# Two looks for the largest scores at a time, in the first and third of every four attention slots of an encoder kernel

## The chip, the cores and the metric

The kernel runs on one core of one Trainium2 chip. The metric is the time of one execution in device microseconds; a kernel's time is the median of several runs. The profiler records one execution with every instruction of the five engines: PE (TensorE), PEld (PE's weight loads), DVE (VectorE), ACT (ScalarE), POOL (GpSimd), and SP, which issues the DMAs.

## The reference, cut to what matters

One layer of a bidirectional encoder is run on two sequences, a prompt of 1024 tokens and a sample of 2048, with width 1024. Behind a normalised input projection stand a pooling mixer, self-attention (8 heads of 64 on 2 key/value heads) and cross-attention (4 heads into 256 memory tokens). Their gated outputs go through one output projection, are normalised and added to x.

```python
def one_block(qblk):
    s = jnp.einsum('bqkgd,bskd->bkgqs', qblk, k, preferred_element_type=jnp.float32) * scale
    p = jax.nn.softmax(s, axis=-1)
    return jnp.einsum('bkgqs,bskd->bqkgd', p.astype(v.dtype), v)
...
mix = jnp.concatenate([pool_out, attn_out, x_out], axis=-1)
y = jnp.einsum('bte,ed->btd', mix, w_out)
return x + rms_norm(y, norm_post)
```

The query and key gains are large, so the softmax needs the largest score of each query before the exponentials are taken.

## The kernel before

The first part (some 700 us) computes all projections and stores queries, keys, values and gates in DRAM. The second part, which the change touches, does attention and output projection. It works through **pairs** of 128-query tiles: 8 pairs of the sample, then 4 of the prompt. A pair has three **groups**, one for each kind: kind 0 and kind 1 are the two key/value heads of self-attention, kind 2 is cross-attention. The order in a pair is 0, 2, 1 (2, 0, 1 in the first). A group goes through its keys in chunks of 128: 16 chunks for self-attention of the sample, 8 for the prompt, 2 for cross-attention. One chunk of one group is a **slot**; there are 344, and `k` is the chunk's number in its group.

PE, ACT, DVE and POOL run in the order in which the loop at the end of the kernel writes the instructions. A slot writes:

- `weights(k, 0)`: the scores S of 512 queries, transposed (keys on partitions), by two matmuls, first from `qa`, then from `qb` (line 220), the second of which also subtracts each query's largest score; ACT takes the exponential P (line 227). S comes from the PSUM pool `pss` with two buffers, P from a pool of six.
- `sums` of the slot before: P is added to the running z, for the sample one half on POOL (line 239) and one on DVE (line 240), for the prompt all of it on DVE.
- one **look** (`largest`, line 191, or 183 for cross-attention): for a later group, the scores of 128 queries against 1024 keys (queries on partitions) go into a buffer N of the PSUM pool `psn`, which has two buffers of 1024 numbers, and DVE reduces it to the negated largest (line 194). 324 looks lie in slots, 20 more in the first part. The last look of a group must be over more than LEAD = 4 slots ahead of the group.
- what is `due` at the slot; `weights(k, 1)` for the other 512 queries; some matmuls of the output projection, if there are any to fill in (`py`, lines 359 to 361); and what is due at the slot plus END = 0.5.

Every fourth slot the **value products** of four chunks stand at the slot's end (`values`, line 252, 16 matmul records): at k = 4, 8, 12 and at the first slot of the next group. Behind a group's last chunk follow, in the slots of the next: `values` at the end of its first slot, `totals` at the end of its second (line 260: the sums of z go into a buffer of `psn`, the same two as the looks'), `take` in its third (line 266: acc times the gate, on DVE) and `inverse` at the end of its third (line 272: DVE reads the totals' buffer, which is held until then).

The lines that set this for the looks and the totals:

```python
psn = ctx.enter_context(tc.tile_pool(name="psn", bufs=2, space=PSUM, side="right", reuse_waits="tile"))
...
at(n + c + 1 + END, g.totals)
at(n + c + 2, g.take)
at(n + c + 2 + END, g.inverse)
```

Here `n` is the group's first slot and `c` its number of chunks.

Of the kernel before, what the change touches and what calls it, by code (L numbers as in the profile page):

```python
# [23 lines left out]
def encoder(ctx, tc, I, O):  # L24
# [375 lines left out]
    LEAD, RUN = 4, 4  # L400
    pairs = [Pair(s, p) for s in (1, 0) for p in range(SEQS[s][1] // 256)]
    groups = []
# [5 lines left out]
    slots = [(g, k) for g in groups for k in range(g.chunks)]  # L408
# [3 lines left out]
    def at(slot, f, *args):  # L412

        later.setdefault(slot, []).append((f, args))

    def due(slot):
        for f, args in later.pop(slot, ()):
            f(*args)  # L418

    first = {}  # L420
# [18 lines left out]
    for g in groups:  # L439
        n, c = first[g], g.chunks  # L440
# [11 lines left out]

    looks, n = {}, len(slots)
    left = {g: list(range(len(g.pieces))) for g in groups}
    while any(left.values()):
        n -= 1
        able = [g for g in groups if left[g] and first[g] - LEAD > n]
        if able:  # L460
            looks[n] = (able[0], left[able[0]].pop())
    ahead = [looks[n] for n in sorted(looks) if n < 0]
    loads = {}
    for n, (g, k) in looks.items():
        if k == 0:
            loads.setdefault(max(n - 3, -1), []).append(g)

    order = {mybir.EngineType.PE, mybir.EngineType.Activation, mybir.EngineType.DVE,
             mybir.EngineType.Pool}

    def look_ahead():

        if ahead:
            g, n = ahead.pop(0)
            g.largest(n)


    with ExitStack() as p1:
# [334 lines left out]
        def groups_of(sb):  # L813
            return mem_groups if SB[sb][0] == "mem" else tok_groups
# [10 lines left out]
        for sb, (kind, s, nb, b0) in enumerate(SB):  # L825
            groups = groups_of(sb)
# [50 lines left out]
    with tc.manual_schedule(engines=order):  # L877
        slot = 0
        while slot < len(slots) or later or fill:
            g, k = slots[slot] if slot < len(slots) else (None, 0)  # L880
            if g:
                g.weights(k, 0)
            if 0 < slot <= len(slots):
                h, kh = slots[slot - 1]
                h.sums(kh)
            for x in loads.get(slot, ()):
                x.load()
            if slot in looks:
                looks[slot][0].largest(looks[slot][1])
            due(slot)  # L890
            if g:
                g.weights(k, 1)
            pauses = sum(x is None for x in fill)
            n = -(-(len(fill) - pauses) // max(1, until[0] - slot - pauses)) if fill else 0
            for _ in range(n):
                x = fill.pop(0)
                if x is None:
                    break
                out, h, c, start, final = x
                out.piece(h, c, start, final)  # L900
                if final:
                    if h == 0 and not out.last:

                        for n in sorted(later):
                            for x in [x for x in later[n] if x[0].__name__ in ("square", "norm", "out")]:
                                later[n].remove(x)
                                x[0](*x[1])
                    at(slot + END, out.half_out, h)
                    at(slot + 1 + END, out.square, h)
                    if h == 1:  # L910
                        at(slot + 2, out.norm)
                        at(slot + 3, out.out)
            due(slot + END)
            slot += 1

# [41 lines left out]
```

## Time and profile before

| | us |
|---|---|
| median of 3 runs (1882.11 to 1884.48) | 1884.24 |
| profiled execution: span from first to last instruction | 1878.7 |
| what lies around the span, by the median | 5.5 |
| second part, from its first S | 699.1 to 1878.7 |
| mean granted TensorE clock | 0.994 |

In the rows of the profile a line (L220) and a tile's name say what an instruction is. "Idle before" is the time for which its engine had nothing to do just ahead of it, with what ended it. A matmul's end is modelled, and matmuls overlap: in a stream, one of 512 columns starts about 0.23 us after the one before, though each shows about 0.40 us. So distances between starts are read here, not durations. One value product of float32 shows as two records.

### The profile page before, as it was taken

To read this page: it belongs to the slowest core of one execution; us is meant where nothing else is said; L and a number is where in the kernel's file an instruction comes from. 1 tells how busy PE (TensorE), PEld (TensorE's weight loads), DVE (VectorE), ACT (ScalarE), POOL (GpSimd) and SP (SyncE) were. 2 spreads that over 40 slices of the span, in tenths; PEclk is the share of its full clock that TensorE was granted. 3 is DMA by queue.
4 is the path that set the end of the run, shared out by engine and by line. 5 is a ranking of instruction groups with operands and counts; after the bars stand their busy time and mean duration, and the time that the engine had idled before them with its cause. 6 is when DMAs were issued, how large, how long until landed. Compare 5 with 4: busy or idle time off the path is not lost. (4 is left out here: it accounts for less than half of the span.)

```text
span 1878.7 us, 23531 instructions
## 1 busy us (share of the span) xinstructions
PE 1813.4 (97%) x8520; PEld 1279.4 (68%) x8520; DVE 1135.6 (60%) x1312; ACT 696.8 (37%) x1266; POOL 846.5 (45%) x748
## 2 busy tenths in 40 slices
PE   7999999999999999999999999999999999999997
PEld 6888888988988884465564656556465655565564
DVE  7745145431544168867768576776858576757744
ACT  5523234222422115444435344443434343333331
POOL 3655016520446007845638374563837452413311
PEclk9999999999999999999999999999999999999998
DMA  7634454254434926212122221212222153223211
GB/s 244 201 113 120 108 162 132 73 154 116 121 99 114 216 65 173 73 27 79 48 79 62 68 62 29 80 45 79 63 68 63 51 137 78 96 85 96 87 43 62
DMA packets 148485, 181.83 MB, mean 97 GB/s; under 512 B 21504, under 2 KB 118416, under 8 KB 148368
## 3 DMA queue, kind: packets, MB, share of 16 engines
q1 hardware_dynamic: 148368, 180.33, 33.9%
q8 instruction: 67, 1.10, 0.3%
q14 instruction: 50, 0.41, 0.1%
HBM read 126.50 MB, written 53.62 MB: 96 GB/s over the span
## 5 line engine op out<-in xcount | busy, mean ns | idle before, releaser
L227 ACT ACTIVATE P<-S 128x512 f32<-128x512 f32 x688 | 399.3, 598 | 555.5 <-PE S L220 430.8
L194 DVE TENSOR_REDUCE nb<-N 128x1 f32<-128x1024 f32 x256 | 311.7, 1218 | 239.8 <-PE N L191 239.0
L239 POOL TENSOR_TENSOR z<-z,P 128x512 f32<-128x512 f32 x224 | 318.4, 1421 | 222.5 <-ACT P L227 217.4
L252 PE MATMUL acc<-P,V 128*64 128x512 f32 (+1 forms) x1472 | 319.4, 576 | 0.5
L220 PE MATMUL S<-qa,KA 128*128 128x512 f32 x640 | 274.6, 429 | 9.7 <-ACT P L227 9.7
L63 POOL TENSOR_TENSOR rs<-rs,mhalf 128x1 f32<-128x1 f32 (+2 forms) x100 | 101.0, 1013 | 401.8 <-DVE rs L61 401.8
L240 DVE TENSOR_TENSOR z<-z,P 128x512 f32<-128x512 f32 (+1 forms) x272 | 271.0, 996 | 13.1 <-ACT P L227 12.9
L220 PE MATMUL S<-qb,KB 65*128 65x512 f32 x640 | 254.0, 397 | 0.0
L550 PE MATMUL pz<-hT_hi,w_hi 128*128 128x512 f32 x592 | 233.1, 394 | 1.3 <-ACT vmst L808 0.8
L552 PE MATMUL pz<-hT_hi,w_lo 128*128 128x512 f32 x592 | 232.1, 392 | 0.5 <-DVE w_lo L69 0.5
L551 PE MATMUL pz<-hT_lo,w_hi 128*128 128x512 f32 x592 | 232.3, 392 | 0.0
L191 PE MATMUL N<-KA,qa 128*128 128x512 f32 x640 | 207.5, 405 | 17.9 <-DVE rz L272 11.2
L252 PEld LDWEIGHTS acc<-P,V 128*64 128x64 f32 x1472 | 98.3, 138 | 178.7 <-issue 169.6
L220 PEld LDWEIGHTS S<-qa,KA 128*128 128x128 f32 x640 | 120.4, 188 | 143.9 <-issue 72.6
L194 DVE TENSOR_REDUCE top<-N 128x1 f32<-128x1024 f32 (+1 forms) x88 | 107.0, 1219 | 94.3 <-PE N L191 74.5
L191 PEld LDWEIGHTS N<-KA,qa 128*128 128x128 f32 x640 | 116.6, 191 | 60.9 <-DVE nb L194 21.9
L550 PE MATMUL pz<-w_hi,hT_hi 128*128 128x384 f32 (+1 forms) x416 | 140.2, 338 | 0.9 <-ACT hT_hi L68 0.8
L551 PE MATMUL pz<-w_lo,hT_hi 128*128 128x384 f32 (+1 forms) x416 | 139.4, 335 | 0.8 <-DVE w_lo L69 0.8
L552 PE MATMUL pz<-w_hi,hT_lo 128*128 128x384 f32 (+1 forms) x416 | 139.7, 338 | 0.0
L359 PE MATMUL py<-wo_hi,mix 128*128 128x512 f32 x352 | 137.7, 391 | 0.0
L360 PE MATMUL py<-wo_lo,mix 128*128 128x512 f32 x352 | 137.7, 391 | 0.0
L361 PE MATMUL py<-wo_hi,mix 128*128 128x512 f32 x352 | 137.4, 390 | 0.0
(120 smaller groups left out, 2479.5 us busy)
## 6 DMA issues: line engine op xcount, KB each, us to landing
wraw<-w_in SPq DMA_DIRECT2D x15, 1536.0 KB
dg<-gst SPq DMA_DIRECT2D x48, 256.0 KB
qa<-dq SPq DMA_DIRECT2D x48, 256.0 KB
gz<-rows SPq DMA_DIRECT2D x72, 128.0 KB
x<-x_sample SPq DMA_DIRECT2D x16, 512.0 KB
xr<-x_sample SPq DMA_DIRECT2D x16, 512.0 KB
y_sample<-xr SPq DMA_DIRECT2D x16, 512.0 KB
dq<-qst SPq DMA_DIRECT2D x96, 64.0 KB
```

The costliest lines, as they stand in the source:

```text
L191: nc.tensor.matmul(S[:, 512 * b:512 * b + 512], lhsT=q, rhs=KA[self.kind][:, k:k + 512], start=True, stop=True)
L194: nc.vector.tensor_reduce(out=out, in_=S, axis=AX.X, op=ALU.max, negate=True)
L220: nc.tensor.matmul(S, lhsT=K[self.kind][rows_, keys], rhs=q, start=n == 0, stop=n == 1)
L227: nc.scalar.activation(out=self.P[k][:, j], in_=S, func=AF.Exp)
L239: nc.gpsimd.tensor_tensor(out=z[:, :cut], in0=a[:, :cut], in1=P[:, :cut], op=ALU.add)
L240: nc.vector.tensor_tensor(out=z[:, cut:], in0=a[:, cut:], in1=P[:, cut:], op=ALU.add)
L252: nc.tensor.matmul(self.acc[64 * j:64 * j + 64, x], lhsT=v, rhs=P[:, j, x], start=(k, i) == (0, 0), stop=k == self.chunks - 1, skip_group_ ...
L359: nc.tensor.matmul(ps, lhsT=mh, rhs=wo_hi[:, c, cols], start=first, stop=False)
L360: nc.tensor.matmul(ps, lhsT=mh, rhs=wo_lo[:, c, cols], start=False, stop=False)
L550: nc.tensor.matmul(ps, lhsT=sh, rhs=mh, start=c == 0, stop=False)
L551: nc.tensor.matmul(ps, lhsT=sh, rhs=ml, start=False, stop=False)
L552: nc.tensor.matmul(ps, lhsT=sl, rhs=mh, start=False, stop=c == n - 1)
```

## The change

The looks no longer stand one in every slot. `room` gives each slot a number of looks by its chunk number: two at k = 0, 4, 8, 12, none at k = 1, 5, ..., two at k = 2, 6, ..., none at k = 3, 7, .... In the slots with k divisible by four the pair stands behind the second S and the output matmuls, directly in front of the value products; in those with k = 2, 6, ... it stands where the one look stood, between the two S. Looks ahead of slot 0 stay one at a time. The number of looks, their matmuls and their reductions are the same, and so is every other instruction; the first part is the same.

```diff
+    def room(n):
+
+        return 1 if n < 0 else (2, 0, 2, 0)[slots[n][1] % 4]
+
     looks, n = {}, len(slots)
     left = {g: list(range(len(g.pieces))) for g in groups}
     while any(left.values()):
         n -= 1
-        able = [g for g in groups if left[g] and first[g] - LEAD > n]
-        if able:
-            looks[n] = (able[0], left[able[0]].pop())
+        for _ in range(room(n)):
+            able = [g for g in groups if left[g] and first[g] - LEAD > n]
+            if able:
+                looks.setdefault(n, []).insert(0, (able[0], left[able[0]].pop()))
...
+    def look(slot):
+
+        for g, n in looks.pop(slot, ()):
+            g.largest(n)
...
-            if slot in looks:
-                looks[slot][0].largest(looks[slot][1])
+            if k % 4:
+                look(slot)
             due(slot)
             if g:
                 g.weights(k, 1)
...
+            look(slot)
             due(slot + END)
             slot += 1
```

On PE, from the totals of the group before (`N<-z,ones`, behind k = 1) to the middle of k = 4, in the third pair of the sample (slots 69 to 72), stood before:

```order
L260 MATMUL N_7699<-z_7359,ones_6117 32x256 x4
L220 MATMUL S_7705<-qa_7076,KA0_5426 128x512
L220 MATMUL S_7705<-qb_7581,KB0_5427 128x512
L191 MATMUL N_7712<-KA1_5428,qa_7533 128x512 x2
L220 MATMUL S_7718<-qa_7076,KA0_5426 128x512
L220 MATMUL S_7718<-qb_7581,KB0_5427 128x512
L220 MATMUL S_7730<-qa_7076,KA0_5426 128x512
L220 MATMUL S_7730<-qb_7581,KB0_5427 128x512
L191 MATMUL N_7736<-KA1_5428,qa_7533 128x512 x2
L220 MATMUL S_7740<-qa_7076,KA0_5426 128x512
L220 MATMUL S_7740<-qb_7581,KB0_5427 128x512
L220 MATMUL S_7745<-qa_7076,KA0_5426 128x512
```

At the same place, on to the value products of k = 4, stands now:

```order
L191 MATMUL N_7712<-KA1_5428,qa_7537 128x512 x2
L191 MATMUL N_7716<-KA1_5428,qa_7537 128x512 x2
L220 MATMUL S_7722<-qa_7090,KA0_5426 128x512
L220 MATMUL S_7722<-qb_7565,KB0_5427 128x512
L220 MATMUL S_7734<-qa_7090,KA0_5426 128x512
L220 MATMUL S_7734<-qb_7565,KB0_5427 128x512
...
L220 MATMUL S_7751<-qa_7090,KA0_5426 128x512
L220 MATMUL S_7751<-qb_7565,KB0_5427 128x512
L191 MATMUL N_7755<-KA1_5428,qa_7537 128x512 x2
L191 MATMUL N_7759<-KA1_5428,qa_7537 128x512 x2
L252 MATMUL acc_7763<-P_7661,V0_6121 64x512 x2
```

Two looks now follow each other with nothing between, and five S (7722, 7734, 7740, 7745, 7751) stand between one pair of looks and the next, where a look stood after every second S.

On DVE, from the first sum of this group (k = 1) on, stood before:

```order
L240 TENSOR_TENSOR z_7709<-P_7661,P_7686 128x512
L194 TENSOR_REDUCE nb_7536<-N_7712 128x1
L266 TENSOR_TENSOR o_7716<-acc_7424,gate_7323 128x512
L272 RECIPROCAL rz_7722<-N_7699 128x256
L240 TENSOR_TENSOR z_7709<-z_7709,P_7704 128x512
L194 TENSOR_REDUCE nb_7536<-N_7736 128x1
```

and stands now:

```order
L240 TENSOR_TENSOR z_7709<-P_7661,P_7690 128x512
L194 TENSOR_REDUCE nb_7540<-N_7712 128x1
L194 TENSOR_REDUCE nb_7540<-N_7716 128x1
L266 TENSOR_TENSOR o_7720<-acc_7428,gate_7327 128x512
L272 RECIPROCAL rz_7726<-N_7699 128x256
L240 TENSOR_TENSOR z_7709<-z_7709,P_7704 128x512
```

Both reductions now stand in front of the reciprocal (`rz<-N`) that reads the totals' buffer; before, one did.

More of the change, by code (lines that the diff above doesn't have):

```diff
@@ L458, in encoder @@
         n -= 1
-        able = [g for g in groups if left[g] and first[g] - LEAD > n]
-        if able:
-            looks[n] = (able[0], left[able[0]].pop())
-    ahead = [looks[n] for n in sorted(looks) if n < 0]
+        for _ in range(room(n)):
+            able = [g for g in groups if left[g] and first[g] - LEAD > n]
+            if able:
+                looks.setdefault(n, []).insert(0, (able[0], left[able[0]].pop()))
+    ahead = [x for n in sorted(looks) if n < 0 for x in looks[n]]
     loads = {}
-    for n, (g, k) in looks.items():
-        if k == 0:
-            loads.setdefault(max(n - 3, -1), []).append(g)
+    for n in looks:
+        for g, k in looks[n]:
+            if k == 0:
+                loads.setdefault(max(n - 3, -1), []).append(g)
     order = {mybir.EngineType.PE, mybir.EngineType.Activation, mybir.EngineType.DVE,
              mybir.EngineType.Pool}
+    def look(slot):
+        for g, n in looks.pop(slot, ()):
+            g.largest(n)
     def look_ahead():
```

## The prediction

> **What bounds the kernel now.** I read the page first: how busy each engine is, and the costliest groups.
>
> ```profile
> span 1878.7 us, 23531 instructions
> PE 1813.4 (97%) x8520; PEld 1279.4 (68%) x8520; DVE 1135.6 (60%) x1312; ACT 696.8 (37%) x1266; POOL 846.5 (45%) x748
> L227 ACT ACTIVATE P<-S 128x512 f32<-128x512 f32 x688 | 399.3, 598 | 555.5 <-PE S L220 430.8
> L194 DVE TENSOR_REDUCE nb<-N 128x1 f32<-128x1024 f32 x256 | 311.7, 1218 | 239.8 <-PE N L191 239.0
> L220 PE MATMUL S<-qa,KA 128*128 128x512 f32 x640 | 274.6, 429 | 9.7 <-ACT P L227 9.7
> L191 PE MATMUL N<-KA,qa 128*128 128x512 f32 x640 | 207.5, 405 | 17.9 <-DVE rz L272 11.2
> ```
>
> PE is busy 97% of the span, and ACT and DVE spend most of their idle time waiting for PE. So what PE loses, the kernel loses, and little on PE is there to win. Next I read PE's waits.
>
> ```profile
> PE N L191 <- DVE rz L272: 11.2, 12, 2.0
> PE S L220 <- ACT P L227: 9.7, 31, 0.8
> PE N L191 <- DVE nb L194: 5.7, 15, 0.9
> PE N L260 <- POOL z L239: 3.9, 2, 3.2
> PE N L183 <- DVE top L194: 2.1, 4, 0.6
> PE S L224 <- ACT P L227: 1.7, 3, 1.2
> ```
>
> Columns: total us, times, longest. Looks wait for their buffer (rz is the reciprocal that frees the totals' buffer, nb and top are reductions): 11.2 + 5.7 + 2.1 = 19.0 us in 31 waits. S waits for ACT: 11.4 us in 34. These are all that a new order of looks could save. Then I read PE in order of time at the third pair of the sample, just behind the totals (0.31 is such a wait).
>
> ```profile
> 906.73 0.50 PE L220 MATMUL S<-qa,KA 128*128 128x512 f32 x1
> 907.07 0.39 PE L220 MATMUL S<-qb,KB 65*128 65x512 f32 x1
> 907.30 0.63 PE L191 MATMUL N<-KA,qa 128*128 128x512 f32 x2
> 907.76 0.40 PE L220 MATMUL S<-qa,KA 128*128 128x512 f32 x1
> 908.00 0.40 PE L220 MATMUL S<-qb,KB 65*128 65x512 f32 x1
> 908.24 0.47 PE L220 MATMUL S<-qa,KA 128*128 128x512 f32 x1
> 908.54 0.39 PE L220 MATMUL S<-qb,KB 65*128 65x512 f32 x1
> 909.25 0.73 PE L191 MATMUL N<-KA,qa 128*128 128x512 f32 x2 [0.31 <-DVE nb L194]
> ...
> 912.64 3.65 PE L252 MATMUL acc<-P,V 128*64 128x512 f32 x16
> ```
>
> From start to start, an S costs PE 0.47 us (907.76 to 908.24), and a look the same (907.30 to 907.76). A wait costs more than its idle column says. From 908.54 to 909.25 there are 0.71 us, where 0.23 is usual: 0.48 for an idle time of 0.31. The rest is 0.16 because the modelled end of a matmul lies beyond the next one's start; a further 0.10 goes when the matmul behind it comes 0.33 later, not 0.23. So I add 0.26 us to each wait.
>
> **Term 1: two looks in one buffer.** `psn` has two buffers. From the end of k = 1 to the end of k = 2 the totals hold one, since the reciprocal is written at the end of k = 2. The pair of looks of k = 2 stands within that time, so both must use the other buffer: the second look's matmuls wait for the first look's reduction. The same holds for a pair in front of the value products of kind 1's first slot, where the totals of the group before kind 2 are still held. Before, a slot's other work lay between two such looks. I count 31 pairs of this sort: three in a usual pair of query tiles, fewer at both ends. DVE there:
>
> ```profile
> 906.93 0.94 DVE L240 TENSOR_TENSOR z<-P 128x512 f32<-128x512 f32 x1
> 907.97 1.22 DVE L194 TENSOR_REDUCE nb<-N 128x1 f32<-128x1024 f32 x1
> ```
>
> The reduction at 907.97 began 0.67 us after its look (907.30), took 1.22, and the look that waited for it began 0.06 later (909.25 after 909.19). So two looks in one buffer start 0.67 + 1.22 + 0.06 = 1.95 us apart, where 0.46 would do: 1.49 us in which PE has nothing, since it runs in the written order. 31 × 1.49 = **+46 us**. In the prompt, where DVE adds all of z ahead of the reduction, some 0.26 more is possible; I add 2 us for its nine pairs. The lower end is nothing, if PE's order left other work there; the rows in the order show none.
>
> **Term 2: runs of S without a look between.** S has two buffers, so each S waits for the exponential of the S two ahead. With a look after every two S there is just time for that. What happens without, the last pair shows, which has no more looks:
>
> ```profile
> 1789.52 0.40 PE L220 MATMUL S<-qa,KA 128*128 128x512 f32 x1
> ...
> 1790.00 0.41 PE L220 MATMUL S<-qa,KA 128*128 128x512 f32 x1
> ...
> 1790.85 0.50 PE L220 MATMUL S<-qa,KA 128*128 128x512 f32 x1 [0.21 <-ACT P L227]
> ...
> 1791.42 0.42 PE L220 MATMUL S<-qa,KA 128*128 128x512 f32 x1
> ...
> 1792.27 0.50 PE L220 MATMUL S<-qa,KA 128*128 128x512 f32 x1 [0.20 <-ACT P L227]
> ...
> 1792.84 0.47 PE L224 MATMUL S<-qa,KA 128*128 128x256 f32 x2
> ```
>
> Five S from 1789.52 to 1792.84 take 3.32 us, not 5 × 0.466 = 2.33: **0.99 us** lost. The first three take 1.90, not 1.40: 0.50 lost; a fourth loses nothing more. In other words, a look between two S was free, and its place is paid for whether a look stands there or not. In the order of before there are three runs of four S, one of six and one of seven; the other runs are of one or two. In the new order I count 39 runs of three, 20 of four, 46 of five, one of six and one of eight. 59 × 0.50 + 46 × 0.99 = 75; the six and the eight add 2.5, and the old ones, which go, took 4: **+73 us**. Where output matmuls fill a slot the run is cut, and this count allows for that. The ends: 36 us, if half of the runs found ACT's exponential done; 85, if copies on ACT fall into the runs.
>
> **Term 3: what goes.** The looks' waits: 19.0 + 31 × 0.26 = **-27 us**, for now a pair of looks has the value products (the row at 912.64, 3.65 us) or a run of five S in front of it, and both are longer than two reductions of 1.22. The waits of S for ACT in the old places: 11.4 + 34 × 0.26 = **-20 us**, taken whole, because term 2 prices the new places whole. The totals' one wait of 3.2 us for POOL, at the first group's end: PE comes later there, so it goes, and with it a stretch at half clock (below): **-5 us**. If none of term 3 goes, the sum is 52 us higher.
>
> **Nothing** I give to the other moves. The value products begin behind a look and not behind an S: same matmuls, same weight loads. ACT's and POOL's order is unchanged. On SP a DMA or two change places with a neighbour. If the looks came too late for the later group's `qb`, S would wait for a DMA; no row of PE's waits names one, and the pairs end earlier than the single looks did.
>
> Sum, against the profiled execution's span: 46 + 2 + 73 - 27 - 20 - 5 = +69 us. With the 5.5 us around the span, which brings 1878.7 to the median of 1884.2, that is **1953 us**, 3.6% slower.
>
> **The clock** may add to it.
>
> ```profile
> 1633.40:1636.80 3.40, 2.05 (x9) 1.02 (x11) 3.40 (x3) 0.64 (x2) 0.14 (x1) 1.00 0.68 242
> 1705.10:1708.50 3.40, 1.56 (x6) 0.87 (x8) 3.40 (x4) 0.86 (x3) 0.64 (x1) 1.00 0.52 179
> 1776.80:1780.20 3.40, 1.67 (x8) 1.15 (x8) 2.12 (x3) 1.54 (x3) 2.81 (x3) 1.00 0.52 154
> 1780.20:1787.00 6.80, 6.18 (x14) 2.40 (x16) 6.36 (x7) 0.60 (x1) 0.60 (x1) 0.50 0.42 128
> ```
>
> After the length come the busy times of PE, PEld, DVE, ACT and POOL, then the granted clock. After stretches with PE busy 1.56 and 1.67 of 3.4 us the clock fell to half; the last row shows it. After one with 2.05 it did not. A stretch of 3.4 us around one stall of 1.49 has PE busy about 2.07 (the modelled end covers 0.16 of the stall), just on the safe side; the prompt's longer stalls are not.
>
> The Trainium skill, "TensorE: Matmul & The Clock Gate", section "Part 1: The HAM clock gate", has the clock halved after an idle window of some 3.4 us; by that, stalls of 1.5 us would cost no clock and the sum would stay as it is. The trace differs: half a window without work was enough here.
>
> **The rivals.**
>
> - *The clock falls at the stalls.* Each fall costs up to 1.7 us, half of 3.4. At all 31 that is 53 us: about 2000. For it: 1.75 us of idle in the prompt reaches the 1.67 row. Against: most stalls lie by 2.05. Chance 0.12 that the time ends over 1985, this or the waits of term 3 staying.
> - *The runs of S are cheaper* because the copies that ACT did among the old waits go elsewhere: half of term 2, 1953 - 36 = 1917. Chance 0.08 for 1900 to 1920.
> - *Only the stalls count,* term 2 being nothing: 1953 - 73 = 1880, about no change. Against it stand the rows at 1790. Chance 0.04.
> - *Faster: the value products hide the reductions and the buffers suffice.* With 3.65 us of value products after a pair, two reductions are free, and the looks' waits go: 1884 - 27 - 5 = 1852. This needs the second look of k = 2 to find a buffer, or PE to have other work in front of it. It decides from the point at which the reciprocal comes before the pair. The order on DVE shows it behind both reductions. Chance 0.06.
>
> **How the numbers follow.** The forecast, 1920 to 1985, has 0.70. The range takes in the cheaper runs at its low end, and at its high end part of the clock and of the waits that stay: 1910 to 1990, with some 0.8. Under 0.2% (3.8 us) a measurement of this kernel can't be told from no change. Faster 0.07, within 0.2% 0.03, slower 0.90.
>
> **What would show it.** Right: PE's wait of N for nb rises from 5.7 us to about 31 × 1.3 = 40 in 31 or more waits (idle column), that for rz nearly goes; S waits for P some 150 times (59 + 2 × 46), some 0.2 us each; in slots without output matmuls, the stretch from one run of value products to the next grows by 1 us or more. ACT's and DVE's durations stay. Wrong: if S's waits don't rise, term 2 falls; if looks wait for rz still, term 3 does; if the mean clock falls below 0.98, the first rival has come.

## The result, and the profile after

| | median us | runs |
|---|---|---|
| before | 1883.2 | 1878.9 to 1884.5 |
| after | 1981.4 | 1978.6 to 1986.5 |

The changed kernel is slower by the ratio 1.0529 (95% interval 1.051 to 1.0549), 98 us. The forecast was 1953, in a range from 1910 to 1990. The profiled execution is the slowest of the four, 1986.5 us.

The page after: span, engines, and the groups shown of before, with the sums on DVE added.

```profile
span 1984.7 us, 23534 instructions
PE 1867.2 (94%) x8520; PEld 1294.9 (65%) x8520; DVE 1223.8 (62%) x1312; ACT 683.6 (34%) x1266; POOL 838.2 (42%) x748
L227 ACT ACTIVATE P<-S 128x512 f32<-128x512 f32 x688 | 386.8, 598 | 676.0 <-PE S L220 438.5
L240 DVE TENSOR_TENSOR z<-z,P 128x512 f32<-128x512 f32 (+1 forms) x272 | 333.7, 1227 | 140.4 <-ACT P L227 134.4
L194 DVE TENSOR_REDUCE nb<-N 128x1 f32<-128x1024 f32 x256 | 303.3, 1215 | 120.1 <-PE N L191 120.0
L220 PE MATMUL S<-qa,KA 128*128 128x512 f32 x640 | 293.2, 458 | 35.6 <-ACT P L227 35.2
L191 PE MATMUL N<-KA,qa 128*128 128x512 f32 x640 | 195.5, 418 | 41.9 <-DVE nb L194 33.3
```

PE's share falls from 97 to 94%, with the same 8520 matmuls. An exponential takes 598 ns and a reduction 1215 (1218 before). Longer are PE's waits, and DVE's sums: 1227 ns against 996, as the same group's row of before shows. The group mixes two shapes; its sums of 512 columns alone rose from 919 to 1175 ns.

```profile
L240 DVE TENSOR_TENSOR z<-z,P 128x512 f32<-128x512 f32 (+1 forms) x272 | 271.0, 996 | 13.1 <-ACT P L227 12.9
```

PE's waits after (total us, times, longest):

```profile
PE S L220 <- ACT P L227: 35.2, 129, 1.2
PE N L191 <- DVE nb L194: 33.3, 23, 3.2
PE N L191 <- DVE top L194: 8.2, 6, 1.4
...
PE N L183 <- DVE top L194: 6.0, 4, 1.5
PE S L224 <- ACT P L227: 3.5, 13, 0.4
...
PE N L260 <- POOL z L239: 0.3, 1, 0.3
```

S waits 142 times, not 34; looks wait 47.5 us, not 19.0, and now for reductions alone. The wait for rz is gone, and that of the totals for POOL fell from 3.9 to 0.3 us. The place in the third sample pair that the prediction read, on PE in order of time (all rows of this kind give start, length and what ran):

```profile
932.30 0.40 PE L220 MATMUL S<-qb,KB 65*128 65x512 f32 x1
932.54 0.62 PE L191 MATMUL N<-KA,qa 128*128 128x512 f32 x2
934.78 0.73 PE L191 MATMUL N<-KA,qa 128*128 128x512 f32 x2 [1.61 <-DVE nb L194]
935.35 0.40 PE L220 MATMUL S<-qa,KA 128*128 128x512 f32 x1
935.59 0.40 PE L220 MATMUL S<-qb,KB 65*128 65x512 f32 x1
935.82 0.40 PE L220 MATMUL S<-qa,KA 128*128 128x512 f32 x1
936.06 0.43 PE L220 MATMUL S<-qb,KB 65*128 65x512 f32 x1
936.67 0.80 PE L220 MATMUL S<-qa,KA 128*128 128x512 f32 x1 [0.18 <-ACT P L227]
937.26 0.63 PE L220 MATMUL S<-qb,KB 65*128 65x512 f32 x1
937.69 0.63 PE L220 MATMUL S<-qa,KA 128*128 128x512 f32 x1
938.12 0.63 PE L220 MATMUL S<-qb,KB 65*128 65x512 f32 x1
938.58 0.80 PE L220 MATMUL S<-qa,KA 128*128 128x512 f32 x1
939.17 0.63 PE L220 MATMUL S<-qb,KB 65*128 65x512 f32 x1
939.60 1.91 PE L191 MATMUL N<-KA,qa 128*128 128x512 f32 x4
941.44 4.46 PE L252 MATMUL acc<-P,V 128*64 128x512 f32 x16
```

Three things are to be seen. The two looks start 2.24 us apart (932.54, 934.78). Five S follow. And from 936.67 on, matmuls start 0.43 us apart, not 0.23: the clock is at half. The busy times of PE, PEld, DVE, ACT and POOL, the granted clock and DMA, in the 3.4 us ahead of that and the 6.8 behind:

```profile
932.90:936.30 3.40, 1.79 (x8) 1.05 (x6) 2.58 (x3) 0.77 (x2) 1.40 (x2) 1.00 0.00 0
936.30:943.10 6.80, 6.62 (x15) 3.53 (x16) 6.70 (x7) 2.67 (x5) 2.55 (x2) 0.50 0.22 70
```

The trace's record of the granted clock shows this once in each usual pair of the sample, at 816.8, 936.3, 1055.7, 1175.2, 1294.7, 1414.1 and 1533.6 us, each time for 6.8 us. In all there are 98 us at half clock, where there were 25 before (8 to 9 us of either lie at the kernel's end, where PE has nothing left to do). A usual pair of the sample takes 119.5 us, not 109.1.

### The profile page after: what moved, and what is told of

Read it like the earlier page. It is cut to its first block, busy times and chain, and to the rows that moved or that the text cites. A ratio compares the mean times of both kernels' runs of the same rounds, so it can differ in the third digit from the quotient of the medians.

```text
span 1984.7 us, 23534 instructions
## 1 busy us (share of the span) xinstructions
PE 1867.2 (94%) x8520; PEld 1294.9 (65%) x8520; DVE 1223.8 (62%) x1312; ACT 683.6 (34%) x1266; POOL 838.2 (42%) x748
## 5 line engine op out<-in xcount | busy, mean ns | idle before, releaser
L227 ACT ACTIVATE P<-S 128x512 f32<-128x512 f32 x688 | 386.8, 598 | 676.0 <-PE S L220 438.5
L239 POOL TENSOR_TENSOR z<-z,P 128x512 f32<-128x512 f32 x224 | 312.3, 1394 | 276.8 <-ACT P L227 272.8
L240 DVE TENSOR_TENSOR z<-z,P 128x512 f32<-128x512 f32 (+1 forms) x272 | 333.7, 1227 | 140.4 <-ACT P L227 134.4
L194 DVE TENSOR_REDUCE nb<-N 128x1 f32<-128x1024 f32 x256 | 303.3, 1215 | 120.1 <-PE N L191 120.0
L220 PE MATMUL S<-qa,KA 128*128 128x512 f32 x640 | 293.2, 458 | 35.6 <-ACT P L227 35.2
L220 PE MATMUL S<-qb,KB 65*128 65x512 f32 x640 | 263.7, 412 | 0.0
L191 PE MATMUL N<-KA,qa 128*128 128x512 f32 x640 | 195.5, 418 | 41.9 <-DVE nb L194 33.3
L191 PEld LDWEIGHTS N<-KA,qa 128*128 128x128 f32 x640 | 124.7, 200 | 84.8 <-DVE nb L194 46.7
L359 PE MATMUL py<-wo_hi,mix 128*128 128x512 f32 x352 | 137.8, 392 | 0.0
L69 DVE TENSOR_TENSOR w_lo<-wraw,w_hi 128x3072 fp32r<-128x3072 f32 (+2 forms) x21 | 67.8, 3227 | 113.1 <-ACT w_hi L68 113.1
```

The source lines that it names most:

```text
L191: nc.tensor.matmul(S[:, 512 * b:512 * b + 512], lhsT=q, rhs=KA[self.kind][:, k:k + 512], start=True, stop=True)
L194: nc.vector.tensor_reduce(out=out, in_=S, axis=AX.X, op=ALU.max, negate=True)
L220: nc.tensor.matmul(S, lhsT=K[self.kind][rows_, keys], rhs=q, start=n == 0, stop=n == 1)
L227: nc.scalar.activation(out=self.P[k][:, j], in_=S, func=AF.Exp)
L239: nc.gpsimd.tensor_tensor(out=z[:, :cut], in0=a[:, :cut], in1=P[:, :cut], op=ALU.add)
L240: nc.vector.tensor_tensor(out=z[:, cut:], in0=a[:, cut:], in1=P[:, cut:], op=ALU.add)
```

## The experiments

Every run is given with the kernel before on the same chip (medians 1882 to 1883 us).

**No shared buffer.** The pairs of looks stay, but not where the totals hold a buffer:

```diff
-        return 1 if n < 0 else (2, 0, 2, 0)[slots[n][1] % 4]
+        if n < 0:
+            return 1
+        g, k = slots[n]
+        if n > 1 and (k in (2, 3) or g.kind == 2 or k < 2 and slots[n - k - 1][0].kind == 2):
+            return 1
+        return (2, 0, 2, 0)[k % 4]
```

> The changed kernel, but no slot in which the totals hold one of the two buffers N gets two looks: k = 2 and k = 3 get one each, as do the slots of cross-attention and the first two behind it. No second look waits for the reduction of the look next to it (31 such places in the changed kernel, 0 here); runs of three S: 49, of four: 17, of five: 33. My theory (each shared buffer costs 1.49 us, and the half-clock stretches come from these stalls): the looks' waits for nb fall from 33 us to under 10 us, half-clock time from 98 us to under 35 us, and the time from 1981 to about 1915 us; the runs of S keep it some 30 us over the kernel before. Rival (the runs of S are nearly all of the loss, the stalls little): 1965 us or more. Rival (the half clock comes from the runs of S): half-clock time stays over 80 us and the time is about 1945 us.

Measured: 1936.9 us, ratio 1.0285 (1.0267 to 1.0302), with 46 us at half clock. PE's waits:

```profile
PE S L220 <- ACT P L227: 33.3, 128, 1.2
PE N L191 <- DVE nb L194: 16.9, 25, 2.2
...
PE N L191 <- DVE top L194: 5.6, 4, 1.5
PE S L224 <- ACT P L227: 3.4, 13, 0.3
PE N L191 <- DVE rz L272: 3.0, 3, 1.0
PE N L183 <- DVE top L194: 2.2, 4, 0.6
```

The shared buffers and what hangs on them are 44 of the 98 us, of which 9 are, by the prediction's prices, fewer and shorter runs of S; the rival by which the stalls are little falls, and so does the one by which the half clock comes from the runs of S. The expected 1915 and the 35 us at half clock were missed: the looks here wait 27.7 us in 36 places and not under 10. Of these, 11.3 us are single looks (19 places), which bring back the old waits; 13.4 us (14 places) are second looks of the pairs in front of the value products, for which DVE was not done with an earlier reduction; 3.0 us are three first looks of such pairs. With these waits as measured, the prediction's prices give 1883, +64 for the runs of S (66 × 0.50 + 33 × 0.99 + 2.5 - 4), -20 for S's old waits and +10 for the looks', 1937. That it meets the measured time is partly luck, as the sum has nothing for the 21 us more at half clock.

**The stall filled.** Work that nobody reads is put into the stall; nothing else moves:

```diff
-        for g, n in looks.pop(slot, ()):
-            g.largest(n)
+        for i, (g, n) in enumerate(looks.pop(slot, ())):
+            if i and held:
+                for _ in range(DUMMY):
+                    nc.tensor.matmul(held[0].zt[:, 512:1024], lhsT=g.qa[:, 0, 0:128],
+                                     rhs=KA[0][:, 0:512], start=True, stop=True)
+            g.largest(n)
```

`held` names the group whose totals hold a buffer (it is set in `totals` and cleared in `inverse`, in lines left out here); DUMMY is 5.

> The changed kernel with five extra matmuls of 512 columns (5 x 0.23 = 1.17 us) between the two looks wherever the totals hold a buffer; they write the unused half of the totals' buffer and nobody reads them. They lie in the stall of 1.49 us, so PE is busy there but nothing else comes earlier. My theory (clock falls because PE stands still in the stalls): half-clock time falls from 98 us to under 40 us and the time from 1981 to about 1950 us, although PE does more work. Rival (a fall of the clock costs nothing, since PE waits anyway): half-clock time falls, the time stays at 1981 us. Rival (the clock falls for another reason, the runs of S): half-clock time and time stay.

Measured: 1961.7 us, ratio 1.0421 (1.0394 to 1.0448). Time at half clock falls from 98 to 15 us. The same place on PE (L192 and L221 are the looks and S, L486 the extra matmuls):

```profile
924.96 0.63 PE L192 MATMUL N<-KA,qa 128*128 128x512 f32 x2
925.42 1.30 PE L486 MATMUL N<-KA,qa 128*128 128x512 f32 x5
927.21 0.74 PE L192 MATMUL N<-KA,qa 128*128 128x512 f32 x2 [0.49 <-DVE nb L195]
927.78 0.39 PE L221 MATMUL S<-qa,KA 128*128 128x512 f32 x1
```

The second look comes no earlier (2.25 us after the first), but S behind it runs at full clock. So **the half clock is 20 us of the loss** (31 were expected), and it comes from the stalls: the runs of S are all still there and alone bring none. **Two matmuls are enough** (DUMMY = 2):

> As the kernel with the filled stalls, with two extra matmuls instead of five (0.47 us of the stall). My theory (the clock falls when about half of 3.4 us is idle): some 1.1 to 1.3 us of idle are left in a stall, too little, so half-clock time stays under 40 us and the time is about 1962 us. Rival (any stall of 1 us brings the fall): half-clock time over 70 us, about 1980 us.

Measured: 1960.6 us, ratio 1.0419 (1.0401 to 1.0436), with 18 us at half clock.

**The third slot's pair alone.** The kernel before, with `room` as in the change but with these numbers, and every look at the old place:

```diff
+    def room(n):
+
+        return 1 if n < 0 else {2: 2, 3: 0}.get(slots[n][1], 1)
```

> The kernel before with one part of the change: two looks in the third slot of each group (k = 2), none in the fourth, one everywhere else at the old place. 22 places with two looks in one buffer, 9 runs of three S and 16 of four, none of five. My theory: 22 x 1.49 = 33 us of stalls and 25 x 0.50 = 12 us of runs, less most of the looks' old waits (27 us): 1900 us, and up to 25 us more if the clock falls in each pair as in the changed kernel: 1900 to 1925 us. Rival (the runs of five S are nearly all of the loss): 1885 us or less.

Measured: 1915.6 us, ratio 1.0167 (1.0151 to 1.0183), within the expected range, with 68 us at half clock. The rival falls: 22 shared buffers without a single run of five S, but with 25 runs of three and four and the half clock that comes with them, cost 33 us. In 15 of the 22 places the second look starts 1.95 or 1.96 us after the first, as forecast, and yet the clock falls in most pairs: the 3.4 us ahead of one fall (912.7 to 916.1) hold such a stall, 1.32 us idle, and a wait of S of 0.21 behind it, and PE is busy 1.91.

**The pair in front of the value products alone.** The changed kernel, with single looks at the old place:

```diff
-        return 1 if n < 0 else (2, 0, 2, 0)[slots[n][1] % 4]
+        if n < 0:
+            return 1
+        g, k = slots[n]
+        if g.kind == 2 or k < 2:
+            return 1
+        return (2, 0, 1, 1)[k % 4]
...
-            if k % 4:
+            if k % 4 or len(looks.get(slot, ())) == 1:
```

> The other part alone: two looks directly in front of the value products at k = 4, 8, 12 and none in the slot behind them; one look in every other slot at the old place, so no two looks share a buffer. 74 runs of three S, 3 of four, none of five; 55 pairs of looks in front of value products. My theory: 74 x 0.50 = 37 us for the runs, less some 10 us of old waits: about 1910 us, with S waiting for P in about 75 places more and half-clock time under 30 us. Rival (runs of S cost nothing, the stalls are all): 1883 us or a little less. Rival (the value products hide the reductions and this pays): 1870 us.

Measured: 1917.8 us, ratio 1.0185 (1.0166 to 1.0203), with 25 us at half clock, as before the change. Behind the value products (PE in order of time):

```profile
1018.40 0.50 PE L220 MATMUL S<-qa,KA 128*128 128x512 f32 x1
1018.74 0.40 PE L220 MATMUL S<-qb,KB 65*128 65x512 f32 x1
1018.97 0.40 PE L220 MATMUL S<-qa,KA 128*128 128x512 f32 x1
1019.21 0.39 PE L220 MATMUL S<-qb,KB 65*128 65x512 f32 x1
1019.82 0.50 PE L220 MATMUL S<-qa,KA 128*128 128x512 f32 x1 [0.22 <-ACT P L227]
1020.16 0.39 PE L220 MATMUL S<-qb,KB 65*128 65x512 f32 x1
1020.39 0.63 PE L191 MATMUL N<-KA,qa 128*128 128x512 f32 x2
```

The third S comes 0.61 us after 1019.21 where 0.23 is usual, and its second matmul 0.34 behind: 0.38 + 0.11, the 0.50 of the prediction. Pairs in front of value products don't pay here; they cost the runs that they leave. S waits in 58 places more (92 against 34), where about 75 were expected. The whole is 8 us over the expected 1910; the looks' waits, of which some 10 us should have gone, grew (29.8 us in 44, against 19.0 in 31). Of them 18.5 us are second looks of 22 of the 55 pairs, which wait for an earlier reduction.

**Free places.** To the kernel with five extra matmuls in the stalls, two more are added between the two S of slots without a look:

```diff
+            if g and g.kind < 2 and k % 2 and slot < 328 and not any(fill) and slot > 8:
+                t = pso.tile([128, 512], F32, name="py", tag="py")
+                for _ in range(2):
+                    nc.tensor.matmul(t, lhsT=g.qa[:, 0, 0:128], rhs=KA[g.kind][:, 0:512], start=True, stop=True)
```

> The kernel with the filled stalls (1962 us), and in 95 slots without looks two more matmuls of 512 columns (0.47 us, as much as a look) between the two S; they write the idle buffer of the output projection, and nobody reads them. That is 95 x 0.47 = 45 us more matmuls on PE. Runs of three S go from 39 to 58, of four from 20 to 13, of five from 46 to 2. My theory (a place between two S is paid for, whether something stands there or not): by the prices of the runs, 37 us of waits go, so about 1970 us; S waits for P some 70 times instead of 160. Rival (the runs of S cost little, and S's waits lie beside others): 1962 + 45 = 2007 us.

Measured: 1969.5 us, ratio 1.0464 (1.0449 to 1.0479). S's wait for ACT among PE's waits, in this kernel:

```profile
PE S L221 <- ACT P L228: 20.9, 75, 1.2
```

and in the kernel with the filled stalls alone:

```profile
PE S L221 <- ACT P L228: 38.8, 147, 1.2
```

PE got 45 us of matmuls and the time rose by 8, as expected. So most of a place between two S is paid for whether a look stands in it or not: this is the price of term 2, shown by filling.

**The reciprocal first.** From the other end: what did the old waits for rz cost? The kernel before, with two functions changed about:

```diff
-        at(n + c + 2, g.take)
-        at(n + c + 2 + END, g.inverse)
+        at(n + c + 2, g.inverse)
+        at(n + c + 2 + END, g.take)
```

> The kernel before, with take and inverse in each other's places: the reciprocal that frees the totals' buffer stands at the third slot's middle, the product of acc and gate at its end. Nothing else is changed. My theory of the old waits: the looks' waits for rz (11.2 us in 12) fall to under 5 us, and the time goes down by some 8 us, to about 1875 us (0.4%). Rival (DVE's queue as a whole is what the looks wait for, so that another wait takes the place): 1883 us.

Measured: 1883.9 us, ratio 1.0002 (0.9991 to 1.0013), no difference. No wait for rz is left, but there is a new one, of value products for `take`, which frees acc:

```profile
PE acc L252 <- DVE o L266: 10.1, 6, 1.7
PE N L191 <- DVE nb L194: 5.7, 15, 0.9
```

The expected 1875 was missed. This is the rival that was named, though the new wait is that of the value products and not of the looks. The code shows where: behind a group that cross-attention follows, the next value products stand at the end of the very slot in which `take` now stands, two slots earlier than behind other groups. So the exchange was made only elsewhere:

```diff
+        follow = groups[g.n + 1:g.n + 2]
+        late = END if follow and follow[0].kind != 2 else 0
-        at(n + c + 2, g.take)
-        at(n + c + 2 + END, g.inverse)
+        at(n + c + 2 + late, g.take)
+        at(n + c + 2 + END - late, g.inverse)
```

> The kernel before with the reciprocal ahead of take as in the run before, but not for a group that is followed by cross-attention, whose value products come one slot later and wait for take. My theory: the new wait of the value products for take (10.1 us in 6, with 0.26 more for each: 12 us) goes, the gain of the reciprocal (11.2 us in 12) stays: about 1873 us, 0.5% under the kernel before. Rival (DVE has no slack at these places, and some other wait takes the place again): 1883 us.

Measured: 1873.9 us, ratio 0.9954 (0.9938 to 0.9969). The largest of the looks' waits that are left:

```profile
PE N L191 <- DVE nb L194: 5.7, 15, 0.9
```

No wait for rz and none for `take` stands among PE's waits any more. This kernel beats both the one before and the changed one.

## Why the prediction was right, and where it was short

The direction, the first two terms and most of the third held; the time came 28 us above the forecast, inside the range.

- **Term 1, the shared buffer** (forecast 46 + 2 us): shown. The 31 second looks start 1.94 us after the first in the 15 cheapest places (1.95 was forecast), 2.03 to 2.26 after it in 15 others, and 3.86 in one; summed over the 31, 51.6 us more than the 0.46 that would do. That 12 of them take 2.2 or more was not foreseen: in the sample the sum on DVE, ahead of the reduction, takes longer there (below).
- **Term 2, the runs of S** (73 us): shown, by the rows of the value-pair run and by the free places. S's waits after, 38.7 us idle in 142 places and 0.26 more for each, are 75.6 us, where the new runs were priced at 77.5. The 4 us of the old runs are taken off twice in the forecast, here and in term 3's 20 us: eight of the 34 old waits of S lie in those runs. Without that slip the sum gives 1957.
- **Term 3, what goes**: right for the looks and for S: no wait for rz is left, and of the looks' 47.5 us in 33 waits 46 lie in the 31 shared buffers. The 5 us at the first group's end did not come. The totals wait for POOL no more, but the stall moved to the second look just behind them, the one 3.86 us after the first: it waits 3.23 us, behind a DVE sum of 2.38, and the clock falls for 6.8 us at 765.6. Nor could the same be expected of the two part kernels, which keep single looks.
- **The step that failed is the clock.** The prediction left it out of the sum because a stretch of 3.4 us around a stall of 1.49 would have PE busy 2.07, "just on the safe side", and gave the fall at the stalls a chance of 0.12 together with other causes. For the 15 cheapest places that held: none of them brought a fall. But in a pair's first group the stall at k = 2 was 0.3 us longer, the stretch had PE busy 1.79, and the clock fell, for 6.8 us at a time; 11 of the 12 longest stalls brought a fall, and one of 2.08. By the prediction's own sign, a mean clock below 0.98, the first rival came: it was 0.976 to 0.979 in the four runs. The filled stalls price it: 20 us of the 98. That is far from the 53 us of that rival's worst case, since 12 of 31 stalls brought a fall.
- Put together: 1961.7 us without the falls, where the forecast without them was 1953; 1981.4 with them. Most of the 9 us between the two are the slip of 4 and the 4 by which term 1 was short.
- Of the other signs, the stretch from the value products at 912.64 to the next grew as named (9.68 us before, 11.80 now), but DVE's durations did not stay.
- The rival by which value products hide the reductions fell: they do hide those of the pair in front of them, but there was little to gain, and the places given up cost more. The rival of the stalls alone fell with the run of the value pair, and that of cheaper runs with S's 75.6 us.

Of the clock rule of the Trainium skill ("TensorE: Matmul & The Clock Gate", "Part 1: The HAM clock gate"), an idle window of some 3.4 us before the clock is halved, this trace says otherwise: 1.6 us without a matmul, in a stretch of 3.4 us, were enough. Where the limit lies is open, and PE's busy time alone does not give it: in the run with the reciprocal first, PE stood still for 1.69 us in one piece and was busy 1.71 of the 3.4 us from 1074.2 to 1077.6, a stretch with value products in place of S, and the clock stayed full.

## What to carry to other kernels

Before work is bundled, ask what it separated: here a look between two S cost little, because S waited for ACT anyway (45 us of matmuls in such places cost 8), and taking it out gave hardly any time back. Two uses of one kind in a row need two free buffers at that place, so count what else holds one there. A stall on PE of 1.3 to 1.6 us, with another wait close by, may cost clock behind it as well; a few matmuls that nobody reads, put into the stall, tell how much (20 us here).

## What the runs showed of the hardware that was not expected

The sum of the first two P on DVE took 1.39 us here, where the same line took 0.94 before the change; DVE and POOL in order of time, at the place shown above:

```profile
931.76 1.28 POOL L239 TENSOR_TENSOR z<-P 128x512 f32<-128x512 f32 x1 [2.19 <-ACT P L227]
932.20 1.39 DVE L240 TENSOR_TENSOR z<-P 128x512 f32<-128x512 f32 x1 [1.50 <-ACT P L227]
933.51 1.21 DVE L194 TENSOR_REDUCE nb<-N 128x1 f32<-128x1024 f32 x1
```

POOL's half of the sum ends at 933.04, DVE's 0.55 us later. Before, POOL's half ran from 906.05 to 907.33 and DVE's sum, begun at 906.93, ended 0.54 us after it. Since the single look's reduction no longer stands in front of it, DVE's sum now begins earlier within POOL's, and takes longer. The whole trace bears this out: 164 sums of 512 columns on DVE began with more than 0.15 us of an instruction of POOL still to run, and each ended 0.55 or 0.56 us after that instruction's end; the 76 that met none running as they began took 0.63 to 0.69 us. Before, 122 began so, and 121 of them ended so. So DVE's sum waits for POOL, and the change made it wait more.

The Trainium skill, "SBUF — State Buffer", section "Who interferes with whom", has an instruction of DVE with two inputs in SBUF wait while a GpSimd instruction that reads SBUF holds the port that both share; the end 0.55 us after POOL's agrees. No run here takes POOL's half away, so that the port is the cause is argued, not shown.

A usual pair of the sample fell to half clock at the same place each time, 119.46 us apart, for 6.8 us of which 2.4 us were lost (119.5 us for the pair, against 117.1 with the stalls filled). But for the last, cut off by the end, the stretches of the clock's record last 3.41 us or a whole multiple, and 119.46 is 35 times that; with the third slot's pair alone, falls lie 112.64 us apart, 33 times. So the clock seems to be set anew on a fixed beat of 3.41 us, and where the beat cuts a stall would decide with its length whether the clock falls; no run here moves a stall against the beat to show it.
